# A two-layer hybrid encoder on one core: the last three gates computed with the activations stationary and turned through memory, and the first two output column groups woven

## The chip, the core and the metric

The kernel runs on one core of a Trainium2 chip. TensorE (PE) multiplies matrices, VectorE (DVE) and ScalarE (ACT) work element by element, GpSimd (POOL) and SyncE (SP) mostly issue DMAs here. The metric is the device time of one execution in microseconds. The kernel before takes 910.96 us, the median of three runs (910.96 to 911.66).

## The reference

Two layers, 256 tokens, width 2048, everything in fp32. Each layer maps its input `x` through one input projection, runs three head groups, multiplies each group's output by a SiLU gate, and maps the concatenation back:

```python
h = x @ w_in
a_q, a_k, a_v, a_z, b_q, b_k, b_v, b_z, b_lr, m_q, m_z = jnp.split(h, cuts, axis=-1)
y_a = chunk_band_attention(heads_a(a_q), heads_a(a_k), heads_a(a_v), rel_table)     # 8 heads, width 1024
o_b = gla_chunk_recurrence(heads_k(b_q), heads_k(b_k), b_v, heads_k(log_g))         # 4 heads, width 512
y_m = memory_attention(heads_m(m_q), heads_m(mk), heads_m(mv))                      # 4 heads into 256 memory tokens, width 512
y = jnp.concatenate([y_a * jax.nn.silu(a_z), y_b * jax.nn.silu(b_z), y_m * jax.nn.silu(m_z)], axis=-1)
out = y @ w_out
x = layer_norm(DEEPNORM_ALPHA * x + out, ln_g, ln_b)
```

`mk` and `mv` are `mem @ w_mem_kv`. The change touches the gates `silu(a_z)` (two groups of 512 columns, called AZ0 and AZ1) and `silu(m_z)` (one group, MZ), the order in which `y @ w_out` is summed, and the loads at the very start.

## The kernel before

**Products in three parts.** A float is split into a rounded part and a remainder (`parts`: ACT writes the rounded part `wh`, line 117, DVE subtracts to get the remainder `wl`, line 118). A product is then three matmuls: high by high, low by high, high by low. Every weight of the projections goes through this split once. Weights come in pieces of 512 KB; four pieces of `raw`, `wh` and `wl` fit at a time (`wp`, four buffers each). So ACT can write the rounded part of a piece as soon as PE has finished the piece four before it, and SP can load a piece's raw weights as soon as DVE has subtracted the piece four before.

**Two ways to lay out a group of 512 output columns.** Each group has 16 blocks of 128 input features, in eight pieces.

- *Activations stationary* (`as_group`, `as_products`): the 128x128 array holds a block of `x`, and the weights stream. Per feature block and per half of the tokens three matmuls of 512 columns: 96 matmuls for a group. The result has tokens on the partitions.
- *Weights stationary* (`ws_group`, `ws_half`): the array holds a block of the weights, and both parts of `x` stream side by side. Per feature block and 128 output columns one matmul of 512 columns and one of 256: 128 matmuls for a group, 64 of each width. The result has features on the partitions, and two sums that `total` adds (ACT line 262, DVE line 263).

What the output projection takes as its stationary operand must have features on the partitions. Before, AZ0, AZ1 and MZ are computed with the weights stationary, so they come out that way round. Groups whose result is wanted the other way round are turned (`turned`): DVE transposes blocks of 32x32 (line 521), POOL issues a DMA of the result to device memory (`home`, line 523), and four DMAs back that place the blocks (line 526), per half of the tokens. So the memory-attention queries (MQ) go before the change already.

**What sets the order.** PE and SP run in the order in which the Python code issues instructions. Heads are generators that yield how many pieces they want to wait; `tick`, called after each piece, resumes those that are due, so that the few matmuls of a head stand between two pieces. `waiting` holds heads that have not begun, `active` at most two or three that have. `finish(gens)` runs the clock until those are done. DVE, ACT and POOL are put in order by a scheduler, each a first-in first-out queue; weight pieces carry a high priority there.

**Around the change.** In each layer, after the gate of the linear attention (BZ), the kernel computes AZ0, AZ1 and MZ. Meanwhile the four heads of memory attention run: scores (`bk<-mk,mq`), a softmax, a turn of the probabilities (`pT`), and the product with the values (`bk<-sc,mv`). Each gate's SiLU (line 897) is multiplied into the head outputs `yraw` (line 901) and split into the operand `yq`. Then four groups of output columns (`WO`, n = 0 to 3) follow, each with pieces 0 to 7, of which pieces 6 and 7 need the operand that MZ gates, and 4 and 5 that of AZ1. The lines of `ln_g` and `ln_b` are loaded by POOL (lines 917 and 918).

Of the kernel before, what the change touches and what calls it, by code (L numbers as in the profile page):

```python
# [36 lines left out]
def hybrid_trunk_kernel(  # L37
# [12 lines left out]
    waiting, active, done, now, linear = [], [], set(), [0], []  # L50
# [39 lines left out]
    def nm(s):  # L90
        uid[0] += 1
        return f"{s}_{uid[0]}"
# [61 lines left out]
    def first_pieces(p, x):  # L154
# [9 lines left out]
        def x_part(j):  # L164
            sp.dma_start(xraw[:, j], xsrc[:, j])  # L165
            parts(x[0][:, j], x[1][:, j], xraw[:, j])
# [4 lines left out]
        if p < 2:  # L171
            with tc.manual_schedule(engines={DVE, mybir.EngineType.Activation}):
                for k in range(2):
                    x_part(slice(j0 + k, j0 + k + 1))
                    cut = 2 if p == k == 0 else 1
                    for h in range(cut):
                        cs = slice(h * 512 // cut, (h + 1) * 512 // cut)
                        sp.dma_start(raws[0][:, k, cs], vsrc[:, k, cs])  # L178
                        split(0, (slice(None), k, cs))
# [12 lines left out]
    def first_memory(mk, mv, each):  # L192
# [6 lines left out]
        def values_of(p, w, kk):  # L199

            for h in range(2 if p == kk == 0 else 1):
                cs = slice(h * 256, h * 256 + 256) if p == kk == 0 else slice(0, 512)
                for t in range(2):
                    as_products(accv[:, t, cs], t, memq, [x[:, :, cs] for x in w], p * 2 + kk, kk, -1 if h else 0)
# [93 lines left out]
    def gla_inputs(l):  # L298
# [5 lines left out]
        for i in range(3):  # L304
            pool.dma_start(raw[i * 16:i * 16 + 16], gate_w[l])  # L305
# [3 lines left out]
        pool.dma_start(gb, gate_b[l])  # L309
        pool.dma_start(ng, norm_g[l])  # L310
# [181 lines left out]
    def gla_turned(yraw, ng, y):  # L492

        yT = []
        for par in range(2):
            yT.append(hd.tile([P, 4, P], F32, name=nm("yT"), tag=("gq", "gk")[par]))
            turned(P, (yT[par], yraw[:, 2 * par:2 * par + 2].rearrange("p t d -> p (t d)")))
            yield 6
        for par in range(2):
# [6 lines left out]
            yield 1  # L506

# [270 lines left out]
    for _ in range(6):  # L778
        mm(idle[:, :P], zeros, zeros, True, True)
# [5 lines left out]
    for l in range(L):  # L785
# [3 lines left out]
        def staged(g, x, raw, place):  # L789
# [4 lines left out]
            active.append((gen, now[0] + 5))  # L794
# [95 lines left out]
        waiting[:0] = gens[0]  # L890
        for i, g in ((1, G_AZ0), (2, G_AZ1), (3, G_MZ)):
            y = operand()
            gates = []
            for j, a, b in ws_group(w512[l, g], xq):
                sz = scratch([P, 2, T])
                total(sz, a, b)
                act.activation(sz, sz, AF.Silu)
                gates.append((j, sz))
            finish(gens[i])
            for j, sz in gates:  # L900
                dve.tensor_tensor(sz, sz, yraw[i][:, j:j + 2], op=ALU.mult)
                parts(y[0][:, j:j + 2], y[1][:, j:j + 2], sz)
            yq.append(y)
# [5 lines left out]
        gb = []  # L909
        rows = norm_rows(l) if last else None  # L910
        for n in range(WO_N):
            if last:
                g, b = scratch([P, 512]), scratch([P, 512])
            else:
                both = per.tile([P, 2, 512], F32, name=nm("gb"), tag=f"yr{n}")
                g, b = both[:, 0], both[:, 1]
            pool.dma_start(g, ln_g[l:l + 1, columns(n)].to_broadcast([P, 512]))
            pool.dma_start(b, ln_b[l:l + 1, columns(n)].to_broadcast([P, 512]))
            gb.append((g, b))
# [28 lines left out]
            acc = as_group(src, yq, 512)  # L948
            for t in range(2):
                add_residual(n, t, acc[:, t], stats)  # L950
            if last:
                r = res[:, 1, columns(n)]
                dve.tensor_tensor(r, r, gb[n][0], op=ALU.mult)
        if not last:
            norm_between(stats)
            gbT = norm_columns(l)
# [86 lines left out]
```

## Time and profile before

| | |
|---|---|
| median of three runs | 910.96 us |
| profiled execution | 911.12 us, of which the span of the trace is 909.3 us |
| granted TensorE clock | 0.998 |
| PE busy | 902.5 us of the span |
| DVE, ACT, POOL busy | 606.7, 486.0, 148.1 us |
| DMA | 200.86 MB, 221 GB/s on the mean |

Times in the trace count from the start of the span. "PE" rows are matmuls; they are pipelined, so two neighbours' durations overlap and the time of one is the step from its start to the next one's start. "PEld" rows are the loads of the stationary operand. The chain of work is followed back from the last instruction, at each step to what released it. A row of an engine ends, in square brackets, with the idle time ahead of it and what ended that.

### The profile page before, as it was taken

To read this page: it belongs to the slowest core of one execution; us is meant where nothing else is said; L and a number is where in the kernel's file an instruction comes from. 1 tells how busy PE (TensorE), PEld (TensorE's weight loads), DVE (VectorE), ACT (ScalarE), POOL (GpSimd) and SP (SyncE) were. 2 spreads that over 40 slices of the span, in tenths; PEclk is the share of its full clock that TensorE was granted. 3 is DMA by queue.
4 is the path that set the end of the run, shared out by engine and by line. 5 is a ranking of instruction groups with operands and counts; after the bars stand their busy time and mean duration, and the time that the engine had idled before them with its cause. 6 is when DMAs were issued, how large, how long until landed. Compare 5 with 4: busy or idle time off the path is not lost.

```text
span 909.3 us, 14115 instructions
## 1 busy us (share of the span) xinstructions
PE 902.5 (99%) x5116; PEld 783.0 (86%) x5116; DVE 606.7 (67%) x865; ACT 486.0 (53%) x708; POOL 148.1 (16%) x279
## 2 busy tenths in 40 slices
PE   9999999999999999999999999999999999999997
PEld 7889998998888888888888899889888888888885
DVE  5765478757566666655587676885756586876566
ACT  5654475474544666533476445754744365663340
POOL 1002002014142232000000220021141431420000
PEclk9999999999999999999999999999999999999999
DMA  8977875668786778756775687666696966696552
GB/s 292 315 229 213 303 222 185 184 206 272 213 238 215 234 221 257 229 197 195 225 249 177 197 242 209 195 195 208 193 282 192 271 208 212 209 295 212 190 162 93
DMA packets 109365, 200.86 MB, mean 221 GB/s; under 512 B 12136, under 2 KB 72936, under 8 KB 109040
## 3 DMA queue, kind: packets, MB, share of 16 engines
q1 hardware_dynamic: 97920, 173.31, 60.5%
q0 software_dynamic: 11232, 26.40, 10.2%
q8 instruction: 40, 0.66, 0.3%
q10 hardware_dynamic: 144, 0.26, 0.1%
q14 instruction: 29, 0.24, 0.1%
HBM read 186.78 MB, written 13.11 MB: 220 GB/s over the span
## 4 chain that ended last, share of the span: by engine, by line
PE 98%; DMA 1%; SPq 0%; DVE 0%; ACT 0%; issue 0%
PE acc L95 90%; PE bk L95 8%; DMA raw<-w 1%; PE bk L615 0%; SPq L178 0%; PE bk L398 0%; SPq L165 0%; ACT res L771 0%; ACT wh L117 0%; DVE stats L756 0%; PE bk L345 0%; SPq L180 0%; DVE res L755 0%; DVE res L707 0%; DVE mvt L710 0%
## 5 line engine op out<-in xcount | busy, mean ns | idle before, releaser
L95 PE MATMUL acc<-wh,x 128*128 128x512 f32 (+2 forms) x1812 | 538.8, 378 | 0.0
L118 DVE TENSOR_TENSOR wl<-raw,wh 128x1024 fp32r<-128x1024 f32 (+3 forms) x321 | 369.4, 1153 | 207.6 <-ACT wh L117 205.7
L117 ACT CAST wh<-raw 128x1024 fp32r<-128x1024 f32 (+3 forms) x321 | 318.5, 994 | 315.2 <-PE acc L95 244.9
L95 PEld LDWEIGHTS acc<-wh,x 128*128 128x128 f32 x1812 | 334.9, 189 | 48.9 <-issue 0.3
L95 PE MATMUL acc<-wl,x 128*128 128x512 f32 (+2 forms) x906 | 340.8, 376 | 0.0
L95 PE MATMUL acc<-x,wh 128*128 128x512 f32 x672 | 212.2, 397 | 0.1
L95 PEld LDWEIGHTS acc<-wl,x 128*128 128x128 f32 x906 | 170.5, 188 | 26.4 <-DVE wl L118 0.6
L95 PEld LDWEIGHTS acc<-x,wl 128*128 128x128 f32 x672 | 126.2, 188 | 29.7
L95 PE MATMUL acc<-x,wl 128*128 128x256 f32 x672 | 132.2, 278 | 0.0
L95 PEld LDWEIGHTS acc<-x,wh 128*128 128x128 f32 x672 | 103.7, 189 | 1.7 <-ACT wh L117 0.5
L523 POOL DMA_DIRECT2D home<-sc x46 | 25.7, 558 | 397.3 <-DVE sc L521 390.6
L526 POOL DMA_DIRECT2D pT<-home x96 | 52.6, 554 | 51.4 <-DMA home<-sc 29.9
L526 POOL DMA_DIRECT2D yr<-home x48 | 26.1, 551 | 15.1 <-issue 8.0
L545 ACT ACTIVATE sc<-sc,mx 128x128 f32<-128x128 f32 (+1 forms) x32 | 14.4, 450 | 17.2 <-DVE mx L543 17.2
L305 POOL DMA_DIRECT2D gwraw<-gate_w x6 | 3.1, 522 | 105.7 <-PE bk L603 104.9
L387 ACT ACTIVATE sc<-sc 128x512 f32<-128x512 f32 x12 | 7.6, 633 | 14.9 <-DVE sc L385 14.9
L521 DVE STREAM_TRANSPOSE sc<-sc 128x384 f32<-128x384 f32 (+1 forms) x24 | 14.9, 619 | 0.5
L538 DVE SCALAR_TENSOR_TENSOR sc<-bk,bias 128x384 f32<-128x384 f32 x16 | 8.7, 544 | 9.1 <-PE bk L95 9.1
L521 DVE STREAM_TRANSPOSE sc<-acc 128x512 f32<-128x512 f32 x18 | 11.8, 696 | 3.6 <-PE acc L95 3.4
L118 DVE TENSOR_TENSOR x<-sc,x 128x512 fp32r<-128x512 f32 x20 | 13.5, 685 | 0.7 <-ACT x L117 0.7
L526 POOL DMA_DIRECT2D qk<-home x24 | 13.1, 552 | 5.0 <-DMA home<-sc 5.0
L118 DVE TENSOR_TENSOR x<-res,x 128x512 fp32r<-128x512 f32 (+2 forms) x14 | 10.5, 765 | 5.1 <-ACT x L117 5.1
(211 smaller groups left out, 601.0 us busy)
## 6 DMA issues: line engine op xcount, KB each, us to landing
raw<-w SPq DMA_DIRECT2D x142, 512.0 KB, 4.4
raw<-w SPq DMA_DIRECT2D x227, 256.0 KB, 4.0
raw<-w SPq DMA_DIRECT2D x64, 388.0 KB, 3.7
home<-sc POOLq DMA_DIRECT2D x30, 256.0 KB, 4.0
bias<-relw SPq DMA_DIRECT2D x16, 192.0 KB, 4.7
yr<-home POOLq DMA_DIRECT2D x48, 64.0 KB, 4.9
home<-sc POOLq DMA_DIRECT2D x16, 192.0 KB, 3.3
pT<-home POOLq DMA_DIRECT2D x64, 48.0 KB, 4.3
```

Of the source, the lines that this page charges most:

```text
L95: pe.matmul(o, l, r, start=start, stop=stop, skip_group_check=True)
L117: act.copy(hi, src)
L118: dve.tensor_tensor(lo, src, hi.bitcast(F32), op=ALU.subtract)
L305: pool.dma_start(raw[i * 16:i * 16 + 16], gate_w[l])
L387: act.activation(dd, dd, AF.Abs)
L521: dve.transpose(blocks.rearrange("p b (g j) -> p g b j", j=32), src.rearrange("p (g b j) -> p g b j", b=4, j=32))
L523: pool.dma_start(homes[-1], blocks)
L526: pool.dma_start(dst[b * 32:(b + 1) * 32], home[:, b].rearrange("(a i) n -> i a n", a=4))
L538: dve.scalar_tensor_tensor(s, pb[:, :384], SCALE, bias[h], op0=ALU.mult, op1=ALU.add)
L545: act.activation(s[:, own[t]], s[:, own[t]], AF.Exp, bias=mx[:, t:t + 1], accum_out=zs[:, t:t + 1])
```

## The change

1. **Gates.** AZ0, AZ1 and MZ are computed with the activations stationary. ACT takes the SiLU straight from the accumulator, one instruction per half of the tokens, then the gate is turned through device memory into a tile `zT`. A new generator `gated` waits until the heads are done, multiplies `zT` by the head outputs (four DVE instructions per group) and splits the result.
2. **Weave.** The output projection's column groups 0 and 1 are summed at the same time, in two accumulators: pieces 0 to 5 of group 0, pieces 0 to 5 of group 1, then pieces 6 and 7 of each. Ahead of piece 2, 4 and 6 of the first group stands a `finish` for the gate that it needs (`need`). In the first layer, the loads of `ln_g` and `ln_b` are written behind the output projection.
3. **`side`.** Generators that place a turned result (`staged`, `gla_turned`, `gated`) go to a list of their own that does not count against the two or three active heads.
4. **The first loads.** The first half of the first weight piece is loaded from ACT's queue, the first activation is rounded by DVE, the first twelve matmuls stand in another order, and seven warming matmuls on zeros stand at the start where there were six.
5. **The loads of the forget gate** (five per layer) go from POOL's queue to SP's.

```diff
     def tick(share=1.0):
 
         now[0] += share
+        for e in [e for e in side if e[1] <= now[0]]:
+            side.remove(e)
+            after = next(e[0], None)
+            if after is not None:
+                side.append((e[0], now[0] + after))
+            else:
+                done.add(e[0])
...
         def x_part(j):
             sp.dma_start(xraw[:, j], xsrc[:, j])
-            parts(x[0][:, j], x[1][:, j], xraw[:, j])
+            if p == j.start == 0:
+                dve.tensor_copy(x[0][:, j], xraw[:, j])
+                dve.tensor_tensor(x[1][:, j], xraw[:, j], x[0][:, j].bitcast(F32), op=ALU.subtract)
+            else:
+                parts(x[0][:, j], x[1][:, j], xraw[:, j])
...
+                    if n == 2:
+                        act.dma_start(raws[0][cuts[k][0]], vsrc[cuts[k][0]])
...
+            if p == kk == 0:
+                (wh, wl), (xh, xl, _) = w, memq[0]
+                for cs in (slice(0, 256), slice(256, 512)):
+                    for i, (a, b) in enumerate(((xh, wh), (xl, wh), (xh, wl))):
+                        for t in range(2):
+                            mm(accv[:, t, cs], a[:, 0, t * P:(t + 1) * P], b[:, 0, cs], i == cs.start == 0, False)
+                return
...
         for i in range(3):
-            pool.dma_start(raw[i * 16:i * 16 + 16], gate_w[l])
+            sp.dma_start(raw[i * 16:i * 16 + 16], gate_w[l])
...
-        pool.dma_start(gb, gate_b[l])
-        pool.dma_start(ng, norm_g[l])
+        sp.dma_start(gb, gate_b[l])
+        sp.dma_start(ng, norm_g[l])
...
+    def gated(zT, yraw, heads, y):
+
+        while not all(h in done for h in heads):
+            yield 1
+        for j in range(0, 4, 2):
+            gz = scratch([P, 2, T])
+            for t in range(2):
+                z, o, r = (zT[:, t].rearrange("p a (k j) -> p k a j", j=32)[:, j:j + 2],
+                           *(x[:, :, t * P:(t + 1) * P].rearrange("p k (a j) -> p k a j", j=32) for x in (gz, yraw[:, j:j + 2])))
+                dve.tensor_tensor(o, z, r, op=ALU.mult)
+            parts(y[0][:, j:j + 2], y[1][:, j:j + 2], gz)
...
-    for _ in range(6):
+    for _ in range(7):
         mm(idle[:, :P], zeros, zeros, True, True)
...
             gen = placed(raw, place)
-            active.append((gen, now[0] + 5))
+            side.append((gen, now[0] + 5))
...
         gens[0] = [gla_turned(yraw[0], gp[2], yq[0])]
-        waiting[:0] = gens[0]
+        side.append((gens[0][0], now[0]))
+        need = {}
         for i, g in ((1, G_AZ0), (2, G_AZ1), (3, G_MZ)):
-            y = operand()
-            gates = []
-            for j, a, b in ws_group(w512[l, g], xq):
-                sz = scratch([P, 2, T])
-                total(sz, a, b)
-                act.activation(sz, sz, AF.Silu)
-                gates.append((j, sz))
-            finish(gens[i])
-            for j, sz in gates:
-                dve.tensor_tensor(sz, sz, yraw[i][:, j:j + 2], op=ALU.mult)
-                parts(y[0][:, j:j + 2], y[1][:, j:j + 2], sz)
-            yq.append(y)
+            acc = as_group(halves(g), xq, 512)
+            yq.append(operand())
+            zT = hd.tile([P, 2, 4, P], F32, name=nm("zT"), tag="qk", bufs=4)
+            sz = [scratch([P, 512]) for _ in range(2)]
+            for t in range(2):
+                act.activation(sz[t], acc[:, t], AF.Silu)
+            turned(P, *((zT[:, t], sz[t]) for t in range(2)))
+            need[i * 2] = [gated(zT, yraw[i], gens[i], yq[i])]
+            side.extend((x, now[0] + 6) for x in need[i * 2])
         finish(gens[0])
...
-            acc = as_group(src, yq, 512)
-            for t in range(2):
-                add_residual(n, t, acc[:, t], stats)
...
+            if n == 0:
+                continue
+            accs = {n: psd.tile([P, 2, 512], F32, name=nm("acc"), tag="acc") for n in ((0, 1) if n == 1 else (n,))}
+            order = [(m, pc) for pcs in (range(6), range(6, 8)) for m in accs for pc in pcs]
+            for m, pc in order:
+                finish(need.pop(pc, ()))
+                w = piece(wo_pieces(l, m)[pc], 512)
+                for kk in range(2):
+                    for t in range(2):
+                        as_products(accs[m][:, t], t, yq, w, pc * 2 + kk, kk)
+                tick()
+                if pc == 7:
+                    for t in range(2):
+                        add_residual(m, t, accs[m][:, t], stats)
```

How the instructions stand on PE at the end of MZ and the start of the output projection, first layer. Each row is one instruction, or several of one form ("x2"), with output, stationary-or-moving inputs and width. Before (`acc_3546` is the second half of MZ, `acc_3673` is column group 0, `x_2943` the operand of its pieces 0 and 1):

```order
1284 L95 MATMUL acc_3546<-x_513,wh_3638 128x512 x2
1285 L95 MATMUL acc_3546<-x_513,wl_3639 128x256 x2
1286 L95 MATMUL acc_3546<-x_513,wh_3638 128x512 x2
1287 L95 MATMUL acc_3546<-x_513,wl_3639 128x256 x2
1288 L95 MATMUL acc_3673<-wh_3675,x_2943 128x512 x2
1289 L95 MATMUL acc_3673<-wl_3676,x_2943 128x512
```

Now (`acc_3423` is MZ, `acc_3637` and `acc_3638` are column groups 0 and 1, `x_3401` is the operand that AZ1 gates):

```order
1282 L102 MATMUL acc_3423<-wh_3596,x_514 128x512 x2
1283 L102 MATMUL acc_3423<-wl_3597,x_514 128x512
1284 L102 MATMUL acc_3637<-wh_3640,x_2944 128x512 x2
1285 L102 MATMUL acc_3637<-wl_3641,x_2944 128x512
...
1330 L102 MATMUL acc_3637<-wh_3730,x_3401 128x512 x2
1331 L102 MATMUL acc_3637<-wl_3731,x_3401 128x512
1332 L102 MATMUL acc_3638<-wh_3758,x_2944 128x512 x2
1333 L102 MATMUL acc_3638<-wl_3759,x_2944 128x512
```

Pairs of 512 and 256 columns became threes of 512, and behind piece 5 of column group 0 comes piece 0 of column group 1, so that twelve pieces stand between MZ and the first piece that its gate feeds, where there were six.

On DVE at the same place, before (`acc_3546` is the second half of MZ, `yr_1027` the output of memory attention, `x_3432` the gated operand; the other rows are remainders of weight pieces):

```order
323 L118 TENSOR_TENSOR wl_3730<-raw_3728,wh_3729 128x1024
324 L263 SCALAR_TENSOR_TENSOR sc_3659<-acc_3546,sc_3659 128x512
325 L118 TENSOR_TENSOR wl_3748<-raw_3746,wh_3747 128x1024
326 L901 TENSOR_TENSOR sc_3659<-sc_3659,yr_1027 128x512
327 L118 TENSOR_TENSOR wl_3766<-raw_3764,wh_3765 128x1024
328 L118 TENSOR_TENSOR x_3432<-sc_3659,x_3432 128x2x256
329 L118 TENSOR_TENSOR wl_3784<-raw_3782,wh_3783 128x1024
```

Now (`sc_3616` is the SiLU of MZ, `zT_3615` its turned form; `wl_3759` and `wl_3777` are the first and second piece of column group 1, the 7th and 8th piece of the weave):

```order
327 L554 STREAM_TRANSPOSE sc_3620<-sc_3616 128x4x4x32
328 L554 STREAM_TRANSPOSE sc_3624<-sc_3617 128x4x4x32
...
331 L125 TENSOR_TENSOR wl_3759<-raw_3757,wh_3758 128x1024
332 L538 TENSOR_TENSOR sc_3747<-zT_3615,yr_1028 128x2x128
333 L538 TENSOR_TENSOR sc_3752<-zT_3615,yr_1028 128x2x128
334 L125 TENSOR_TENSOR wl_3777<-raw_3775,wh_3776 128x1024
335 L125 TENSOR_TENSOR wl_3795<-raw_3793,wh_3794 128x1024
336 L538 TENSOR_TENSOR sc_3747<-zT_3615,yr_1028 128x2x128
337 L538 TENSOR_TENSOR sc_3752<-zT_3615,yr_1028 128x2x128
338 L125 TENSOR_TENSOR wl_3813<-raw_3811,wh_3812 128x1024
```

The gate's products now wait for a DMA (`zT`), and remainders of weight pieces are queued behind them.

On POOL, between the turn of the third memory head and that of MZ, first layer, before (`pT` are probabilities, `yT` the linear attention's result, `gb` the lines of `ln_g` and `ln_b`):

```order
59 L526 DMA pT_3263<-home_3266 32x4x128 x4
60 L523 DMA home_3314<-sc_3312 128x512
61 L523 DMA home_3416<-sc_3414 128x512
62 L917 DMA gb_3670<-ln_g 128x512
63 L918 DMA gb_3670<-ln_b 128x512
64 L526 DMA pT_3311<-home_3314 32x4x128 x4
65 L526 DMA yT_3413<-home_3416 32x4x128 x4
```

Now (`zT_3402` is the turned AZ1; `gb_4262` overwrites the head outputs that the products of AZ0 read):

```order
61 L556 DMA home_3290<-sc_3288 128x512
62 L559 DMA pT_3242<-home_3245 32x4x128 x4
63 L944 DMA gb_4262<-ln_g 128x512
64 L944 DMA gb_4262<-ln_b 128x512
65 L559 DMA pT_3287<-home_3290 32x4x128 x4
66 L556 DMA home_3409<-sc_3407 128x512
67 L556 DMA home_3413<-sc_3411 128x512
68 L559 DMA zT_3402<-home_3409 32x4x128 x4
```

The gates' turns joined the queue, and the fourth memory head's probabilities (`pT_3287`) now stand behind two loads that wait for AZ0's products.

More of the change, by code (lines that the diff above doesn't have):

```diff
@@ L912, in hybrid_trunk_kernel @@
             if last:
[L913 to L919, printed above, removed]
+                gb.append((scratch([P, 512]), scratch([P, 512])))
+                load_norm(n)
             src = wo_pieces(l, n)
@@ L947, in hybrid_trunk_kernel @@
                 break
[L948 to L953 removed]
+            if n == 0:
[10 more added lines that the diff above has]
+                if pc == 7:
+                    for t in range(2):
+                        add_residual(m, t, accs[m][:, t], stats)
+                    if last:
+                        r = res[:, 1, columns(m)]
+                        dve.tensor_tensor(r, r, gb[m][0], op=ALU.mult)
         if not last:
+            for n in range(WO_N):
+                both = per.tile([P, 2, 512], F32, name=nm("gb"), tag=f"yr{n}")
+                gb.append((both[:, 0], both[:, 1]))
+                load_norm(n)
             norm_between(stats)
```

24 lines of the change are left out of this document (14 added, 10 removed).

## The prediction

> **What bounds the kernel now.** I read the page first (span, busy times, clock, chain), then what PE waited for, then the chain in order of time around the gates.
>
> ```profile
> span 909.3 us, 14115 instructions
> PE 902.5 (99%) x5116; PEld 783.0 (86%) x5116; DVE 606.7 (67%) x865; ACT 486.0 (53%) x708; POOL 148.1 (16%) x279
> PEclk9999999999999999999999999999999999999999
> PE 98%; DMA 1%; SPq 0%; DVE 0%; ACT 0%; issue 0%
> PE bk L95 <- DVE eps L784: 1.1, 1, 1.1
> PE bk L95 <- ACT nparts L117: 0.3, 1, 0.3
> PE bk L759 <- DVE nt L721: 0.3, 1, 0.3
> ```
>
> PE is busy from end to end at the full clock, the chain is 98% PE, and all that PE's list of waits shows is 1.7 us at the very start and end. So a change in this kernel is worth what it takes off PE's stream, less whatever wait it opens in it. The profiled execution took 911.12 us around its span of 909.3; the median of the runs, 910.96, is 0.16 lower. A difference under 0.2%, 1.8 us, is about what a measurement here can't tell from none.
>
> **The gates on PE.** Two stretches of the chain hold nothing but one layout each: 128 matmuls of a gate with the weights stationary, one whole group, and 84 with the activations stationary.
>
> ```profile
> 252.53 19.06 PE acc L95 x84
> 329.13 22.29 PE acc L95 x128
> 351.42 0.72 PE bk L95 x6
> 354.93 0.85 PE bk L95 x6
> 355.77 114.26 PE acc L95 x515
> ```
>
> A group costs 22.29 us with the weights stationary. With the activations stationary a matmul steps 19.06 / 84 = 0.227 us, so a group of 96 costs 21.78, and a piece (12) 2.72. The gain is 0.51 us a group; three groups in two layers make **3.1 us**. The long last row agrees (48 of its matmuls are still the old layout, 8.36 us; the other 467 step 0.227), so the bounds of this term are narrow, 2.9 to 3.2. Where the half microsecond comes from can be seen in the steps:
>
> ```profile
> 330.36 0.63 PE L95 MATMUL acc<-x,wh 128*128 128x512 f32 x2
> 330.82 0.40 PE L95 MATMUL acc<-x,wl 128*128 128x256 f32 x2
> 331.05 0.63 PE L95 MATMUL acc<-x,wh 128*128 128x512 f32 x2
> L95 PEld LDWEIGHTS acc<-x,wl 128*128 128x128 f32 x672 | 126.2, 188 | 29.7
> ```
>
> Two matmuls of 512 take 0.46 us and two of 256 take 0.23: 0.23 and 0.115 each. Columns streamed are the same in both layouts (64 x 512 + 64 x 256 = 96 x 512); there are 32 fewer instructions a group, and each costs some nanoseconds beside its columns.
>
> Two rules of the Trainium skill would make this another number. Its page "TensorE: Matmul & The Clock Gate", section "Back-to-back issue gap", gives columns / 2.4 + 2.5 ns per warm matmul: 20.80 us for the old group and 20.72 for the new, an estimate from that page, so 0.5 us over all six groups. It speaks against the change, and the rows step longer than it says (230 and 227 ns where it has 216). The same page's Part 3, "The mechanism", lets a weight load run beside a matmul only on other rows of the array; with the 188 ns of the row above, 32 fewer loads would then be worth 6.0 us a group, 36 us in all. The rows speak against it: a matmul and its 188 ns load together step 227 ns, so the loads lie beside the matmuls.
>
> **What the gates cost elsewhere.** The nearest relative of a turned gate is the turn of the queries (MQ) before, with 2 transposes, 2 + 8 POOL DMAs and the same sizes. MQ's last matmul is the 60th of the 84 above: 252.53 + 60 x 0.227 = 266.15. Then:
>
> ```profile
> 266.19 1.31 DVE L521 STREAM_TRANSPOSE sc<-acc 128x512 f32<-128x512 f32 x2 [0.59 <-PE acc L95]
> 267.20 1.16 POOL L523 DMA_DIRECT2D home<-sc  x2 [2.11 <-DVE sc L521]
> 271.94 4.36 POOL L526 DMA_DIRECT2D yr<-home  x8 [3.58 <-issue]
> 278.92 0.62 ACT L117 CAST mq<-yr 128x512 fp32r<-128x512 f32 x1 [2.79 <-DMA yr<-home]
> 282.57 0.62 ACT L117 CAST mq<-yr 128x512 fp32r<-128x512 f32 x1
> 358.01 0.69 DVE L901 TENSOR_TENSOR sc<-sc,yr 128x512 f32<-128x512 f32 x1 [0.70 <-ACT sc L897]
> 358.94 1.23 DVE L118 TENSOR_TENSOR wl<-raw,wh 128x1024 fp32r<-128x1024 f32 x1 [0.24 <-ACT wh L117]
> 357.34 0.63 ACT L897 ACTIVATE sc<-sc 128x512 f32<-128x512 f32 x1 [1.14 <-DVE sc L263]
> ACT wh L117 <- PE acc L95: 244.9, 173, 2.1
> ```
>
> The first half was there 12.8 us after the last matmul, the second by 16.4. A gate adds ahead of it two SiLUs (1.3 us) and perhaps one remainder in front on DVE (1.2), and behind it four products (1.4) and two splits (2.7): about 23 us. For MZ the weave gives 12 pieces x 2.72 = 32.7 us until its operand is needed, so 9 us are over; AZ1 has MZ's eight pieces and four more, the same, and AZ0 more. So the weave by itself gains nothing (PE did not wait for memory attention), but it is the cover: with six pieces, 16.3 us, a turned MZ would be 7 us late in each layer. Per group ACT loses two multiplications and DVE two additions of `total`, about what the transposes add. ACT spent 244.9 us waiting for PE to free weight buffers, so there is room. POOL gets 5.5 us more per gate, on 148 busy of 909. I cost this at zero, with the two places where the cover is thinnest for the range.
>
> *Place one: DVE's queue, MZ in the first layer.* The products of the first half stand behind the remainder of the 7th piece of the weave. ACT can write a piece when PE has ended the one four before, so DVE gets there at 3 x 2.72 + 1.0 + 1.2 = 10.4 us after MZ's end and waits until 1.3 + 1.2 + 12.8 = 15.3; two products (0.7) and the remainder of the 8th piece (1.2) end at 17.2. PE wants it after seven pieces, at 19.1. That leaves 1.9 us. In the second layer the products stand two pieces further back and 7.3 are left.
>
> *Place two: POOL's queue, the fourth memory head in the first layer.* Its probabilities were the tightest thing before:
>
> ```profile
> 343.21 1.66 POOL L526 DMA_DIRECT2D pT<-home  x3 [3.54 <-DMA home<-sc]
> 347.25 0.56 POOL L526 DMA_DIRECT2D pT<-home  x1 [2.38 <-issue]
> 353.78 0.71 ACT L117 CAST sc<-pT 128x256 fp32r<-128x256 f32 x2 [3.18 <-DMA pT<-home]
> ```
>
> They landed at 353.78, and the six matmuls that use them took 0.85 instead of 0.72: a stall of 0.13 us. Now two loads that wait for AZ0's products stand in front. I count from BZ's end. AZ0 ends at 22.4, its products by 22.4 + 2.5 + 16.4 + 1.4 = 42.7, the two loads take 1.1 and the four reads 2.2, and the last lands 6.0 later (347.81 to 353.78): 52.0. PE wants the head at 58.7 (AZ0, AZ1 and four pieces of MZ, 20 x 2.72, with 4.3 of small matmuls between), and ACT reaches the cast only when PE has ended the third piece of MZ, at 55.3: after one `wh` (1.05), the cast, a remainder and a subtraction, at 58.5. So 0.2 us are left and I take 0, with -0.1 (the old stall gone) to +0.6 (a late remainder in both layers).
>
> The pieces of the gates are now two DMAs of 256 KB instead of one of 512, as those of BZ and MQ are already; SP waits there for buffers, not for its own issues. The loads of the forget gate add five issues to SP per layer; the first layer's stand ahead of a load that had to wait for a buffer anyway:
>
> ```profile
> SPq L142 <- DVE wl L118: 366.8, 167, 5.3
> POOL gwraw L305 <- PE bk L603: 104.9, 1, 104.9
> ```
>
> The second row is POOL standing at the forget gate's load until PE freed its buffer, for 104.9 us, at a time when nothing else was asked of it. SP comes to that load only with the group behind, when PE is long past it. Zero, with up to 0.3 us if the issues delay a piece.
>
> **The start.**
>
> ```profile
> 0.74 0.39 SPq L165 DMA_DIRECT2D res<-memT  x1
> 1.05 2.93 PE L95 MATMUL bk<-zeros 128*128 128x128 f32 x12 [1.05 <-DVE eps L784]
> 1.18 0.89 SPq L178 DMA_DIRECT2D raw<-w  x2
> 3.92 0.50 PEld L95 LDWEIGHTS acc<-wh,x 128*128 128x128 f32 x2 [0.24 <-ACT wh L117]
> 10.04 0.30 PEld L95 LDWEIGHTS acc<-x,wh 128*128 128x128 f32 x2 [0.54 <-ACT wh L117]
> 12.36 0.19 PEld L95 LDWEIGHTS acc<-wl,x 128*128 128x128 f32 x1 [0.43 <-DVE wl L118]
> 0.00:12.00 12.00, 10.83 (x48) 9.39 (x48) 4.66 (x12) 5.99 (x11) 3.48 (x11) 1.00 0.78 247
> 12.00:24.00 12.00, 12.00 (x60) 9.82 (x59) 9.40 (x12) 8.78 (x12) 0.00 (x0) 1.00 1.00 346
> ```
>
> PE is held up by data until 12.4 us. Taking one of the two first weight loads off SP brings all behind it forward by 0.89 / 2 = 0.45 us. At most it is that shift and what the five POOL loads cost that leave this time (they were issued over about 3 us, with the DMA engines 0.78 busy here against 1.00 after: 0.66), together 1.1; at least nothing, if the transfers and not their issue set the pace, which 1.00 busy right after suggests. The seventh warming matmul adds 2.93 / 6 = 0.5 us ahead of the first real one, which now has its data 0.4 earlier; it delays the start by some 0.2 but leaves less to stall for later, so it counts as zero, bounds 0 to +0.3. I take **-0.4 us**, nearest to the shift that SP's row shows.
>
> **Sum.** -3.1 (gates) - 0.4 (start) + 0 (the rest) = -3.5: a span of 905.8, a profiled execution of 907.6, and from the median 910.96 - 3.5 = **907.5 us**. Its own range: 906.5 (gates -3.2, start -1.1, the old stall of 0.1 gone) to 909.1.
>
> **The rivals.**
>
> *DVE's queue blocks the weights (slower).* If a turned half comes later than 12.8 us after its matmuls, every microsecond beyond the 1.9 left at place one stops PE, since the remainders behind the product can't pass it. To lose the 3.5 us and 1.8 more, the half must come 1.9 + 5.3 = 7.2 us later, at 20.0. Then the first layer stands still for 5.3 us: 912.8; at 8 us later 913.6 to 914, the second layer joining past 7.3. For it: POOL has more to do just there, and idle times of 3.5 us in its rows above. Against it: MQ's turn ran beside a full DMA load too. 6 in 100.
>
> *A small stall and no gain at the start.* The half comes 3 to 4 us later, or a fourth head's subtraction is late in both layers: 1 to 2 us lost, nothing won at the start. 910.96 - 3.1 + 1.7 = 909.6; from 909.1 to 911. For it: 0.2 and 1.9 us are thin margins. 16 in 100, a third of it still faster by 0.2%.
>
> *The layout is worth nothing.* Only columns count, and they are the same: the start alone, 0.4: 910.6. Against it the two rows of the chain, which measure whole groups. 4 in 100. The Trainium skill's issue gap is all but this case: by its 0.5 us the time would be 910.1.
>
> *The weight loads count in full.* If the 188 ns of a load were added to each matmul, 32 x 6 loads less would be 36 us, with the start 874.5. Against it PE's steps of 227 ns for matmul and load. 1 in 100. The Trainium skill's rule on row groups, above, makes this case.
>
> **How the numbers follow.** The forecast has 73 in 100. Faster by over 0.2% (below 909.1): 73 + 1 + 5 = 79. Within: 11 + 4 = 15. Slower: 6. The range takes in the forecast's own and most of the small stall: 906.5 to 909.8.
>
> **What would show it.** Matmuls `acc<-x,wh` of 512 columns fall from 672 to 288; a gate group takes 21.8 us in the chain; PE's list of waits stays at under 2 us beside the start; the two waits of PEld at 10.04 and 12.36 come some 0.4 us earlier or vanish. DVE shows one wait of about 5 us for `zT` in the first layer's weave, with no wait of PE behind it. I'd be wrong if PE waits on `wl` there, if gaps appear ahead of `bk<-sc,mv` or the first piece fed by MZ, or if a new gate group takes 22.3 us.

## The result, and the profile after

| | before | after |
|---|---|---|
| median | 911.64 us (6 runs, 910.96 to 912.34) | 907.69 us (6 runs, 907.30 to 909.65) |
| ratio | | 0.996, interval 0.9948 to 0.9973 |
| profiled execution, its span | 911.12, 909.3 | 907.30, 905.5 |

The change makes the kernel faster by 0.4%, about 4 us. The same lines of the page as were shown of before (span, busy times, chain, what PE waited for), now of the changed kernel:

```profile
span 905.5 us, 13967 instructions
PE 898.8 (99%) x4926; PEld 773.8 (85%) x4926; DVE 605.4 (67%) x878; ACT 480.3 (53%) x695; POOL 176.0 (19%) x329
PE 99%; DMA 0%; DVE 0%; ACT 0%; issue 0%
PE bk L102 <- DVE eps L817: 1.1, 1, 1.1
...
PE acc L102 <- ACT wh L124: 0.2, 1, 0.2
L102 PE MATMUL acc<-x,wh 128*128 128x512 f32 x288 | 91.1, 398 | 0.0
```

PE is still the chain from end to end, and no wait of any size has opened. POOL is busier by 28 us. The 384 matmuls `acc<-x,wh` of the three gates in two layers are gone (672 to 288).

The chain in order of time (start, length, what), first of before, then of after: the first steady row, the end of BZ and the first pieces of AZ0, a whole gate group, the stretch from the fourth memory head of layer 1 to layer 2's first steady row, pieces beside a head's small matmuls, and the row ahead of the end.

```profile
50.98 57.84 PE acc L95 x300
...
799.95 2.79 PE acc L95 x16
...
888.04 11.09 PE bk L95 x60
```

```profile
50.03 57.84 PE acc L102 x300
...
288.46 19.08 PE acc L102 x84
...
324.86 21.81 PE acc L102 x96
...
350.89 122.44 PE acc L102 x540
...
496.36 57.85 PE acc L102 x300
...
764.29 2.76 PE acc L102 x12
...
793.78 2.77 PE acc L102 x12
...
884.40 11.09 PE bk L102 x60
```

Of the 3.8 us between the two spans, 0.95 are there at the first steady row (50.98 to 50.03), 2.69 come between that row and the last (837.06 us to 834.37), and 0.2 behind it. The 2.69 include the old stall of 0.13.

### The profile page after: what moved, and what is told of

Read it like the earlier page. It is cut to its first block, busy times and chain, and to the rows that moved or that the text cites. A ratio compares the mean times of both kernels' runs of the same rounds, so it can differ in the third digit from the quotient of the medians.

```text
span 905.5 us, 13967 instructions
## 1 busy us (share of the span) xinstructions
PE 898.8 (99%) x4926; PEld 773.8 (85%) x4926; DVE 605.4 (67%) x878; ACT 480.3 (53%) x695; POOL 176.0 (19%) x329
## 4 chain that ended last, share of the span: by engine, by line
PE 99%; DMA 0%; DVE 0%; ACT 0%; issue 0%
PE acc L102 90%; PE bk L102 8%; PE bk L648 0%; DMA raw<-w 0%; PE bk L419 0%; ACT res L804 0%; DVE stats L789 0%; PE bk L366 0%; DVE res L788 0%; ACT wh L124 0%; DVE res L740 0%; DVE mvt L743 0%; PE bk L792 0%; ACT nparts L124 0%; DVE rs_u L751 0%
## 5 line engine op out<-in xcount | busy, mean ns | idle before, releaser
L102 PE MATMUL acc<-wh,x 128*128 128x512 f32 (+2 forms) x2196 | 656.2, 380 | 0.2 <-ACT wh L124 0.2
L102 PEld LDWEIGHTS acc<-wh,x 128*128 128x128 f32 x2196 | 405.5, 188 | 63.4 <-ACT wh L124 0.5
L102 PE MATMUL acc<-wl,x 128*128 128x512 f32 (+2 forms) x1098 | 414.7, 378 | 0.0
L102 PEld LDWEIGHTS acc<-wl,x 128*128 128x128 f32 x1098 | 205.9, 188 | 34.0 <-DVE wl L125 0.4
L102 PE MATMUL acc<-x,wh 128*128 128x512 f32 x288 | 91.1, 398 | 0.0
L102 PEld LDWEIGHTS acc<-x,wl 128*128 128x128 f32 x288 | 54.1, 188 | 12.6
L102 PE MATMUL acc<-x,wl 128*128 128x256 f32 x288 | 56.7, 278 | 0.0
L102 PEld LDWEIGHTS acc<-x,wh 128*128 128x128 f32 x288 | 44.8, 189 | 1.3 <-ACT wh L124 0.2
L559 POOL DMA_DIRECT2D zT<-home x48 | 26.2, 553 | 32.8 <-DMA home<-sc 17.6
L554 DVE STREAM_TRANSPOSE sc<-sc 128x512 f32<-128x512 f32 (+1 forms) x36 | 22.6, 642 | 1.9 <-ACT sc L931 1.4
L578 ACT ACTIVATE sc<-sc,mx 128x128 f32<-128x128 f32 (+1 forms) x32 | 14.4, 449 | 17.2 <-DVE mx L576 17.2
```

What stands on the lines that cost most here:

```text
L102: pe.matmul(o, l, r, start=start, stop=stop, skip_group_check=True)
L554: dve.transpose(blocks.rearrange("p b (g j) -> p g b j", j=32), src.rearrange("p (g b j) -> p g b j", b=4, j=32))
L559: pool.dma_start(dst[b * 32:(b + 1) * 32], home[:, b].rearrange("(a i) n -> i a n", a=4))
L578: act.activation(s[:, own[t]], s[:, own[t]], AF.Exp, bias=mx[:, t:t + 1], accum_out=zs[:, t:t + 1])
```

## The experiments

Times are medians; before ran beside each set of kernels, with 911.89, 911.89 and 911.90 us.

| kernel | time, us | ratio to before, interval |
|---|---|---|
| start alone (parts 4 and 5) | 910.64 | 0.9985, 0.9975 to 0.9996 |
| first loads alone (part 4) | 911.33 | 0.9994, 0.9985 to 1.0002 |
| forget gate's loads alone (part 5) | 910.75 | 0.9991, 0.9982 to 0.9999 |
| gates alone (parts 1 to 3) | 912.90 | 1.0010, 1.0001 to 1.0020 |
| gates and part 5 | 909.91 | 0.9980, 0.9971 to 0.9989 |
| gates, layer norm loads on SP | 909.37 | 0.9976, 0.9967 to 0.9985 |
| changed kernel without the weave | 922.09 | 1.0117, 1.0102 to 1.0133 |
| changed kernel again | 907.58 | 0.9956, 0.9944 to 0.9969 |
| changed, layer norm loads on SP | 907.78 | 0.9961, 0.9949 to 0.9974 |
| changed, MZ's product later in the code | 907.64 | 0.9955, 0.9942 to 0.9969 |
| changed, MZ's blocks written twice | 907.80 | 0.9960, 0.9948 to 0.9973 |
| changed, both margins wider | 908.91 | 0.9965, 0.9953 to 0.9978 |

**The two halves, each alone.** Before with parts 4 and 5 of the change:

```diff
+                dve.tensor_copy(x[0][:, j], xraw[:, j])
...
+                        act.dma_start(raws[0][cuts[k][0]], vsrc[cuts[k][0]])
...
-        pool.dma_start(ng, norm_g[l])
+        sp.dma_start(ng, norm_g[l])
...
-    for _ in range(6):
+    for _ in range(7):
```

> The kernel before with the new start alone (first loads, order of the first matmuls, seventh warming matmul, forget-gate loads on SP); gates and output projection as before. Reading of the two traces: the stream of matmuls from 17 us on stands 0.94 us earlier after the change than before, so 0.9 us faster than before, 910.7 against 911.6. The prediction's own size: 0.4 us. If the earlier stream is an accident of one execution: no change.

And the changed kernel with those parts undone, so gates, weave and `side` alone:

```diff
-        sp.dma_start(ng, norm_g[l])
+        pool.dma_start(ng, norm_g[l])
...
-    for _ in range(7):
+    for _ in range(6):
```

> The changed kernel with the old start: gates with the activations stationary, turned, woven output columns. If a gate's gain is its layout alone: 6 x 0.51 = 3.1 us faster than before by the prediction; 2.5 to 2.7 by the two traces, which show 0.48 a group, less what small matmuls between the pieces cost. If only columns count: no change. Together with the start alone it should make the 3.8 us between the two kernels.

The start alone gained 1.25 us, the gates alone lost 1.0. Together they gain 4, so the parts don't add up. What PE waited for, with the gates alone, and POOL's, ACT's and DVE's rows at the memory heads of layer 1:

```profile
PE bk L102 <- ACT sc L124: 2.3, 1, 2.3
PE bk L102 <- DVE sc L125: 1.0, 1, 1.0
```

```profile
324.40 2.28 POOL L545 DMA_DIRECT2D zT<-home  x4 [6.20 <-PE acc L102]
326.67 0.56 POOL L317 DMA_DIRECT2D ng<-norm_g  x1
329.47 2.19 POOL L545 DMA_DIRECT2D zT<-home  x4 [2.24 <-issue]
337.78 0.54 POOL L930 DMA_DIRECT2D gb<-ln_g  x1 [5.02 <-DVE sc L524]
...
338.85 3.82 POOL L545 DMA_DIRECT2D pT<-home  x7
336.72 0.76 DVE L524 TENSOR_TENSOR sc<-zT,yr 128x256 f32<-128x256 f32 x2 [3.25 <-DMA zT<-home]
348.50 0.71 ACT L124 CAST sc<-pT 128x256 fp32r<-128x256 f32 x2 [5.46 <-DMA pT<-home]
```

This is the forecast's place two. The next layer's `norm_g`, still loaded by POOL here, stands between the two halves of AZ0's read-back; the second half is late, DVE's product of it (336.72) is late, the two layer norm loads wait for that product (337.78), and behind them stand the probabilities of two memory heads. In the changed kernel only the fourth head stands behind those loads, and `zT` is read in one go (323.33):

```profile
323.33 4.37 POOL L559 DMA_DIRECT2D zT<-home  x8 [5.47 <-issue]
334.75 2.20 POOL L559 DMA_DIRECT2D pT<-home  x4
336.94 0.57 POOL L944 DMA_DIRECT2D gb<-ln_g  x1
338.89 1.66 POOL L559 DMA_DIRECT2D pT<-home  x3 [0.81 <-DMA home<-sc]
348.79 0.71 ACT L124 CAST sc<-pT 128x256 fp32r<-128x256 f32 x2 [1.17 <-DMA pT<-home]
349.23 0.76 DVE L125 TENSOR_TENSOR sc<-pT,sc 128x256 fp32r<-128x256 f32 x2 [0.34 <-ACT sc L124]
350.16 0.73 PE bk L102 x6
```

Two kernels test that reading by opening the lock in two ways. Gates and part 5:

```diff
-            pool.dma_start(raw[i * 16:i * 16 + 16], gate_w[l])
+            sp.dma_start(raw[i * 16:i * 16 + 16], gate_w[l])
...
-        pool.dma_start(gb, gate_b[l])
-        pool.dma_start(ng, norm_g[l])
+        sp.dma_start(gb, gate_b[l])
+        sp.dma_start(ng, norm_g[l])
```

> The new gates with the old start, as in the run before, but with the forget gate's five small loads of each layer on SP instead of POOL (one part of the change's start). Theory A: the 4 us that the gates alone lost in layer 1 came from POOL's queue, where the load of the next layer's norm_g stood between the two copies that read back zT of the fourth gate group, and the two layer norm loads behind it waited for DVE's product of that zT and held the copies of the third and fourth memory head. Without norm_g the order of POOL there is the changed kernel's: the waits of PE for ACT's sc (2.3 us) and DVE's sc (1.0 us) go, and the time is 909.0 us (908.3 to 909.8), 2.6 below before. Theory B: the gates gain only together with the earlier first loads of the start; then the time stays at 912 to 913 us and the waits of 2.3 and 1.0 us stay.

Gates with `norm_g` left on POOL, but layer 1's layer norm loads moved:

```diff
-                pool.dma_start(dst, src[l:l + 1, columns(n)].to_broadcast([P, 512]))
+                (pool if last else sp).dma_start(dst, src[l:l + 1, columns(n)].to_broadcast([P, 512]))
```

> The new gates with the old start, but with layer 1's eight layer norm loads on SP instead of POOL; the load of norm_g stays on POOL between the two copies of zT. Theory A, with the layer norm loads as the lock: the copies of the two memory heads no longer stand behind DVE's product, the waits of 2.3 and 1.0 us go, and the time is 909.0 us (908.3 to 909.8) even though DVE still waits about 3 us for the second half of zT. If norm_g alone is the lock (it makes the copies late whatever stands behind), 911.5 to 913 us and a PE wait for ACT's sc of at least 1 us.

Both waits went in both kernels, and the times fell by 3.0 and 3.5 us against the gates alone. So the lock is POOL's order, and the start's other part has nothing to do with it. Of the five loads, `norm_g` is the one that stood in that stretch of the queue. In the second kernel the fourth head's cast starts without a wait, 3.5 us before the changed kernel's. It pays for that later: the eight loads stand on SP ahead of the second layer's weights, and PE waits there.

```profile
345.28 0.71 ACT L124 CAST sc<-pT 128x256 fp32r<-128x256 f32 x2
...
L930 SPq DMA_DIRECT2D gb<-ln_g x4: 430/732/1034, 431.7 to 435.8; - x4
PE acc L102 <- DVE wl L125: 1.1, 2, 0.5
351.47 78.18 PE acc L102 x345
499.45 57.85 PE acc L102 x300
```

From the end of the fourth head to layer 2's first steady row this kernel takes 147.98 us; the changed kernel takes 145.47. That is 2.5 us given back. The same move made in the changed kernel, where it opens a place that is not shut:

> The changed kernel with layer 1's eight layer norm loads on SP. Theory A: there the loads held the fourth head's copy by 1 to 2 us, within its cover; taken away, only PE's 0.3 us wait beside it can go: 907.4 us (906.9 to 907.8), no measurable difference from the changed kernel. If POOL's queue still cost the changed kernel more than its PE waits show, 906.5 or less. If SP's queue, waiting for the last gate products with these loads, holds the next layer's first weights, slower than 908.5 and PE waits for ACT wh at the start of layer 2.

It measured 907.78 us (907.42 to 909.12), no difference that five runs could show. The trace has both sides of the move. From the first steady row to the end of the fourth head this kernel takes 300.85 us and the changed kernel 300.86, so place two costs the changed kernel nothing. From there to layer 2's first steady row it takes 146.11 us instead of 145.47: the loads on SP give back 0.6.

```profile
50.41 57.84 PE acc L102 x300
351.26 86.87 PE acc L102 x383
```

Gates and part 5, at 909.91, still missed the upper end of its expectation, 909.8, by a little. Its trace shows why: its last transfer.

```profile
902.71 2.17 ACTq L749 DMA_DIRECT2D out<-res  x1
q14 instruction: 1, 0.01, 0.7%
885.57 11.09 PE bk L102 x60
```

ACT's last issue took 2.17 us, in the changed kernel 0.35, and the span ends 22.5 us after the row of 60 matmuls starts instead of 21.1. From 902 to 906 us the queue that carries instructions moved a packet (second row); before and the changed kernel have none in that stretch. The gates alone have both the packet and the long issue (2.39 us); the twelve other profiles, before and after among them, have 0.35 to 0.38. So both kernels lose 1.3 to 1.5 us at their ends in the execution that was profiled, most likely to an instruction fetch there; the two things came together both times, but no run separates them. Set against part 5 alone (910.75), the gates gain 0.8 and, if this 1.3 is in most executions, 2.1; the chain of that kernel says 2.70 (834.56 against 837.26 us).

**The start, split.** The first loads alone (part 4), and part 5 alone:

> As the start alone, but with the forget-gate loads still on POOL. If the first loads and the order of the matmuls make the gain: the same 0.9 us faster than before. If the five POOL loads were what slowed the transfers (the prediction's upper bound put up to 0.66 us on them): no more than 0.3 to 0.4 us faster, and the rest comes with their move.

> The kernel before with only the forget gate's five small loads of each layer on SP instead of POOL. If these loads cost the start nothing and the old layer 1 nothing: 911.6 us, within 0.3 of before. If moving them is what made the whole start faster than its other half (which gave 0.6 us of 1.2): 911.0.

Part 4 gave 0.6 us, not sure to differ from nothing, and part 5 1.1 (0.1 to 1.6), where I had expected nothing at the start. At the start part 5 shows nothing beyond the scatter: its first steady row is at 50.74 (before 50.98), and the one execution of it that was profiled took 911.16, as before's. What differs is the upper end: before's 27 runs beside it reach from 910.25 to 913.97, part 5's eleven from 910.17 to 911.22. Before has the same `norm_g` on POOL among the layer norm loads, so a lock that closes in some executions would fit; no profiled execution of before shows it, so that stays argued.

**The weave.** The changed kernel with one column group at a time:

```diff
-            if n == 0:
-                continue
-            accs = {n: psd.tile([P, 2, 512], F32, name=nm("acc"), tag="acc") for n in ((0, 1) if n == 1 else (n,))}
+            accs = {n: psd.tile([P, 2, 512], F32, name=nm("acc"), tag="acc") for n in (n,)}
```

> The changed kernel with the column groups of the output projection one after the other, as before, so that six pieces (16.3 us) stand between MZ and the first piece that its gate feeds. If the weave is the cover that the turn needs: the operand is there 23 us after MZ by the prediction's count, 24 to 26 by the trace after, so PE waits 7 to 10 us in each layer, 14 to 20 us slower than the changed kernel. If the weave is not needed: the same as the changed kernel within 1 us.

```profile
PE acc L102 <- ACT x L124: 7.9, 2, 4.8
PE acc L102 <- DVE x L125: 0.9, 2, 0.6
```

It lost 14.4 us, and PE waits for the gated operand `x`. So the weave is the cover. But those waits are 8.8 us of the 14.4: 5.4 in the first layer and 3.4 in the second, where 7 to 10 in each were expected. Here is the first layer, with PE's granted clock (the 0.50) in one of the stretches behind the wait:

```profile
383.03 0.78 PE L102 MATMUL acc<-wh,x 128*128 128x512 f32 x1 [4.78 <-ACT x L124]
386.75 1.05 PE L102 MATMUL acc<-wh,x 128*128 128x512 f32 x2
387.61 0.63 PE L102 MATMUL acc<-wl,x 128*128 128x512 f32 x1
386.00:388.00 2.00, 2.00 (x6) 0.50 0.90 313
```

Behind the wait a matmul of 512 columns steps 0.86 / 2 = 0.43 us instead of 0.227, until 390. The second layer shows the same after a wait of 3.2 us, for a shorter time (837.4 to 840.5). The 20 slow matmuls of both layers cost some 4 us more than they would at full clock. That is most of what the waits leave.

**Place one.** The changed kernel again, beside three that were to move the margin at MZ's product. In the first the code makes the product due two pieces later, which was to put one more subtraction of weights ahead of it on DVE in layer 1:

```diff
-            side.extend((x, now[0] + 6) for x in need[i * 2])
+            side.extend((x, now[0] + (8 if i == 3 else 6)) for x in need[i * 2])
```

> The changed kernel, unaltered, beside the three kernels that follow, so that they are compared on one chip. 907.7 us, between 907.3 and 909.7; PE's waits in the two layers' weaves 0.3 us in all.

> The changed kernel with the memory gate's product due two pieces later (place one): in layer 1, DVE has one more subtraction of weights ahead of that product, so that 2.7 us more lie between the last prepared piece and PE's need. If place one costs the changed kernel nothing, as its profile says (0.2 us left): 907.7 us, no difference from it. If it stalls in a part of the runs, and so makes the run of 909.65: the same lowest time of 907.3 and none above 908.2.

In the second, MZ's turned blocks are written twice:

```diff
-            pool.dma_start(homes[-1], blocks)
+            [pool.dma_start(homes[-1], blocks) for _ in range(1 + again)]
```

> The changed kernel with the memory gate's turned blocks written to DRAM twice (the second write stands behind the first in POOL's queue, and the reading back waits for it; the numbers do not change). This makes zT some 2 to 5 us later in both layers. Theory (place one): in layer 1, where 0.2 us are left, DVE holds the subtractions of weights behind the product, and PE waits as long as zT is later, less 0.2 us; in layer 2, with some 7 us left, nothing: 909.5 to 912.5 us, with PE waits for DVE's wl in layer 1 alone. Rival (pieces already prepared carry PE over it): 907.7 us.

The third has the later product and layer 1's layer norm loads on SP:

> The changed kernel with both margins widened: layer 1's layer norm loads on SP, and the memory gate's product due two pieces later. 907.3 us (906.9 to 907.7): what the two remaining places cost is 0.3 us of PE waits, so hardly better than the changed kernel; 906.5 or less if waits that the profile of one execution does not show cost more.

The later product moved nothing. In its trace all five engines run the same instructions in the same order as in the changed kernel, and in layer 1 the product stands behind the same subtraction (371.46 and 379.41 us there, 370.87 and 378.91 in the changed kernel). The scheduler had put it there already. So this kernel is one more repeat of the changed one (907.28 to 907.89). In the same way the last kernel runs the order of the changed kernel with the loads on SP, and repeats that one. It missed its expectation of at most 907.7.

Taken together, the sixteen runs of the changed kernel's order have a median of 907.6 us, and the one of 909.65 stays alone. The ten runs with the loads on SP have 908.4, and five of them took 908.9 or more. So those loads, ahead of layer 2's weights, cost about 0.8 us, in a part of the executions (PE waited 0.7 us for `wl` there in the one of 908.98).

The doubled write was meant to stall layer 1 and did not (907.80). DVE there, in the changed kernel and with the doubled write:

```profile
370.87 1.22 DVE L125 TENSOR_TENSOR wl<-raw,wh 128x1024 fp32r<-128x1024 f32 x1 [1.45 <-ACT wh L124]
378.91 0.76 DVE L538 TENSOR_TENSOR sc<-zT,yr 128x256 f32<-128x256 f32 x2 [6.82 <-DMA zT<-home]
379.58 2.35 DVE L125 TENSOR_TENSOR wl<-raw,wh 128x1024 fp32r<-128x1024 f32 x2
383.66 1.29 DVE L125 TENSOR_TENSOR x<-sc,x 128x512 fp32r<-128x512 f32 x2
```

```profile
371.11 1.22 DVE L125 TENSOR_TENSOR wl<-raw,wh 128x1024 fp32r<-128x1024 f32 x1 [1.45 <-ACT wh L124]
373.83 1.23 DVE L125 TENSOR_TENSOR wl<-raw,wh 128x1024 fp32r<-128x1024 f32 x1 [1.50 <-ACT wh L124]
381.53 0.76 DVE L538 TENSOR_TENSOR sc<-zT,yr 128x256 f32<-128x256 f32 x2 [6.47 <-DMA zT<-home]
```

The product did come 2.6 us later, but the scheduler, which sees the second write, put one more subtraction (373.83) ahead of it, and a piece lasts 2.72 us on PE. The delay moved the order along with it. So neither this run nor the later product says anything against a lock at place one, and none of the runs shows that lock; a delay that the scheduler doesn't see was not tried.

No version tried beats the changed kernel.

## Why the prediction was right, and where not

- **The time.** 907.5 was forecast, 907.69 and 907.58 came. Much of that is luck: the forecast gain of 3.5 us was taken from 910.96, the median of three runs, and more runs of before have 911.6 to 911.9. Measured against those, the gain is 4.0 to 4.3. What the profiled pair and the mean of the starts show adds up to less, about 3.3: 2.7 between the first and the last steady row, 0.5 at the start, 0.2 at the end. The other 0.6 to 1.0 stands in no profiled execution. Part 5's 1.1 on before would fill it, but its cause is only argued above.
- **Gates, -3.1: the sign right, the size not.** A gate group in the chain takes 21.81 us, close to the 21.78 forecast; the 0.03 makes 0.2 in six groups. But between the first and last row of the chain only 2.69 us came off, 0.13 of it the old stall: 2.56 for six groups, below the bound of 2.9. The term was priced from undisturbed stretches. A piece beside a head's small matmuls costs 2.79 in the old layout, a plain eighth of 22.29; in the new one it costs 2.76 to 2.77 where a plain piece has 2.72 or 2.73. Four such and a pair (5.48) make 0.2 us a layer, and the six small matmuls between them take 0.72 to 0.73 instead of 0.71 to 0.72. So a small matmul between pieces costs the new layout something that it did not cost the old. The prediction also laid the gain to 32 instructions fewer a group. Before's rows don't show that: from 330 to 350 us a matmul of 512 columns steps 0.233 us on the mean and one of 256 steps 0.115, half of it, so nothing is left for an instruction as such. Both are slower for their columns than the new layout's 0.227; why, no run shows.
- **Start, -0.4: right as a mean, by one execution too small.** The profiled pair differs by 0.95. In the thirteen profiles whose chain shows it, the first steady row stands at 50.98, 50.74, 50.37, 51.01 and 50.61 with the old start (mean 50.74) and at 50.03, 50.36, 49.82, 50.41, 50.33, 50.28, 50.51 and 50.45 with the new (50.27): 0.47. The two waits of weight loads at 10.04 and 12.36 are gone, as one of the signs said; two of 0.2 and 0.4 us stand at 6.57 and 8.67 instead. The first weight load's move and the seventh warming matmul were not told apart.
- **The forget gate's loads, 0: the step that failed.** I asked what the five loads cost SP, and not what they do on POOL. With them left there the same gates are 3.0 us slower (912.90 against 909.91), place two being closed, and moving them alone gave before 1.1 us (0.1 to 1.6).
- **Place two, POOL's queue: the place and the margin right, the path not.** I had the fourth head's remainder done 0.2 us ahead of PE. It ends at 349.99 and PE uses it at 350.16. But I had the last read landing 52.0 us after BZ's end and ACT's own order as the limit. BZ ends with the first piece of the row at 288.46, at 288.46 + 12 x 0.227 = 291.2. ACT was ready at 347.6, as counted, and then stood 1.17 us for the landing, until 348.79, 57.6 after BZ. The reads were all issued by 341.7 instead of 337.2, since POOL had the head's own write and the third head's reads in front (2.8 us) and then waited 1.4 us for that write and a read; and the last took 7 us to land, not 6. The subtraction ended 58.8 us after BZ and PE came at 59.0, for 58.5 and 58.7 in the count. So the 0.2 us is partly luck. The old stall is gone (0.73 for six matmuls, not 0.85). With one load more in that queue it shuts, for 3.0 us. It was the thin place.
- **Place one, DVE's queue: the mechanism unproven, the size off.** MZ ends at 350.89 + 48 x 0.227 = 361.8. Its first half was multiplied at 378.91, 17.1 us later, not 15.3, and DVE stood 6.8 us, not 5. The next subtraction ends 19.0 us after MZ, PE wants it at 19.1: 0.1 us left of the 1.9. The term that failed is the turn: POOL's reading back began 6.5 us after the write was issued, for MQ 4.7.
- **The cover: right, its price by luck.** MZ's operand was forecast 23 us after MZ; DVE ends it at 384.9, 23.1 after. Without the weave it was to be 7 us late in each layer, and 7.2 a layer were lost. But PE got going again 6.4 us late in the first layer (384.46 instead of 378.1) and 4.0 in the second (837.36 instead of 833.3); the halved clock behind the waits, which the forecast did not have, made up the rest.
- **Layout worth nothing, weight loads in full: neither.** The chain's 21.81 excludes the first. By the Trainium skill's "Back-to-back issue gap" (TensorE: Matmul & The Clock Gate), whose formula the page gives for a single matmul by itself, six groups save 0.5 us, an estimate from that page; the traces say 2.6. By the rule that the Trainium skill's Part 3 on the same page ("The mechanism") lists under what overlaps, which the prediction weighed, 36 would have gone; the same section also lets a load go ahead into a background weight buffer, and the measured 2.6 decides against the rule.

## What to carry to other kernels

Before moving work through a queue that only issues DMAs, write down what each entry of that queue waits for: one small load between two reads, with two more loads behind them, held back eight reads and cost 3 us, more than the gates gain. Price a layout both in an undisturbed stretch and beside the small work that is woven into it: the second gave back 0.3 to 0.4 us of the 3.1 forecast. Where a scheduler sets the order, a delay that it can see is no test of a margin, and the order in the trace tells whether an edit moved anything: two of the kernels here ran the order of another. And a wait of PE of 3 us or more costs more than its length, as the next section shows.

## What the runs showed of the hardware that was not expected

**TensorE's first microseconds.** Some of the first twelve matmuls of 256 columns, in one execution of the gates alone, then of gates with part 5. Both have the first loads of before.

```profile
4.97 0.40 PE L102 MATMUL acc<-wh,x 128*128 128x256 f32 x2
5.21 0.28 PE L102 MATMUL acc<-wl,x 128*128 128x256 f32 x1
```

```profile
6.51 0.63 PE L102 MATMUL acc<-wh,x 128*128 128x256 f32 x2
6.94 0.41 PE L102 MATMUL acc<-wl,x 128*128 128x256 f32 x1
```

From one row to the next a matmul steps 0.24 / 2 = 0.12 us in the first, and 0.43 / 2 = 0.215 in the second. PE works at half speed first and doubles at a moment that differs: by 5.0 us in the one, not yet at 6.9 in the other. The granted clock in the profile's windows reads 1.00 there all the while. The Trainium skill (TensorE: Matmul & The Clock Gate, "What's actually happening") states a half rate until one window of about 3.4 us has been busy, in windows that run on regardless of the kernel's start; the doublings here, 3.9 and about 6.1 us after the first warming matmul (1.05 us), agree with it. The first steady rows of the two executions differ by 0.64 us (50.37, 51.01), but not by the doubling alone: at 10 us they are 0.18 apart, and the rest comes up to 12.7 us, where the second waits for weights. So half a microsecond at the start can't be judged from one execution of each kernel.

**TensorE's clock behind a wait.** Without the weave, PE sat idle for 4.8 us in the first layer and for 3.2 in the second. Behind both, the granted clock read 0.50 (384 to 388 us, 838 to 840) and matmuls took nearly twice their time, for some 6 and 3 us. With the gates alone PE sat idle for 2.3 us ahead of a head's matmuls and the clock read 1.00 throughout. No run has an idle time between 2.3 and 3.2 us. Here the granted clock shows the half rate that it doesn't show at the start.

**A packet of an instruction queue** beside the last issue came with 1.3 to 1.5 us more at the end of two kernels, as shown above, though the issue itself is the same instruction in all of them. That the one caused the other is not shown.
